# The causal mask of an attention's scores: from a matrix product to a vector addition, with five small edits elsewhere

## The chip, the cores and the metric

One core of a Trainium2 chip runs the whole kernel. The metric is device time in microseconds (us) of one execution, start to end. A core has a matrix engine (TensorE, "PE" in the profile; its weight loads are "PEld"), a vector engine (VectorE, "DVE"), a scalar engine (ScalarE, "ACT"), a general engine (GpSimd, "POOL") and a queue for transfers (SyncE, "SP"). They run side by side and each takes its own instructions in order; semaphores hold an instruction back until what it needs is there. Products are written into eight banks of an accumulator memory, each 128 partitions by 512 float32; the banks are read by VectorE and ScalarE.

## The reference

A decoder layer on 512 tokens of width 1024, in float32: a layer norm of the input, two token mixers side by side (a gated linear attention, GLA, and a multi-head latent attention, MLA), gates and an output projection, a layer norm (LN1), a dense block with a squared ReLU, and a last layer norm (LN2). The change is mainly in the MLA's scores:

```python
for blk in range(seq // Q_BLOCK):                     # 4 blocks of 128 queries
    q0, q1 = blk * Q_BLOCK, (blk + 1) * Q_BLOCK
    s = (jnp.einsum('bhqd,bhkd->bhqk', q_nope[:, :, q0:q1], k_nope[:, :, :q1])
         + jnp.einsum('bhqr,bkr->bhqk', q_rope[:, :, q0:q1], k_rope[:, :q1]))
    s = s.astype(jnp.float32) * scale
    mask = (q0 + jnp.arange(Q_BLOCK))[:, None] >= jnp.arange(q1)[None, :]
    p = jax.nn.softmax(jnp.where(mask, s, -jnp.inf), axis=-1).astype(v.dtype)
    outs.append(jnp.einsum('bhqk,bhkv->bhqv', p, v[:, :, :q1]))
...
h = layer_norm(DEEPNORM_ALPHA * h + mix, ln1_g[l], ln1_b[l])
ff = jnp.square(jax.nn.relu(h @ w_ff1[l])) @ w_ff2[l]
h = layer_norm(DEEPNORM_ALPHA * h + ff, ln2_g[l], ln2_b[l])
```

There are 8 heads, with 128 columns without and 64 with rotation. Only the last 128 columns of a block's scores, its own diagonal, need a mask.

## The kernel before

To keep the precision of float32, each operand of a product is split into a high part and a residual (names ending in hi and lo, or h and l), and a product is made of three: high x high, high x low, low x high. `split` (L109) makes an operand's parts: ScalarE copies the high part, VectorE subtracts it from the source. Weights go through `fetch` (DMA on SyncE's queue into `wraw`) and `pump` (L177), which splits the next weight tile on ScalarE (L189) and VectorE (L190); `weights` calls `pump` ahead of its use. `gemm_fm` (L245 to L247) and `gemm_tm` (L278 to L280) are the products; at half of their evictions `gemm_tm` also calls `pump` for the next matrix (L292, L293).

The order on each engine is not written out by hand. The program is recorded as a stream with generators (`spawn`, `tick`, `finish`) that interleave side work with the products, and a scheduler with a timeline model then fixes the order of each engine. `tc.issue_after(x)` makes an instruction stand behind x in that order.

The stages that the change touches, with their lines:

- Head. `load_x` brings the first two blocks of 128 token rows; `ln_rows` (L400) makes mean and inverse deviation (`bn_stats` L403, `bn_aggr`, a power on GpSimd L406) and normalises: block 0 on ScalarE with one activation of 1024 columns (L410, after `nmr` on VectorE, L409), block 1 on VectorE (L412). `ln_transpose` (L414) transposes 128x128 pieces on TensorE (L421) into banks and applies gain and bias (L424, L426, L428), which gives `h`, the operand of every projection.
- Queries. `mla_qr` (L813) projects four heads' rotary parts with `gemm_tm`; `ev_qr` evicts each of four row blocks by `rope` (three VectorE operations, L498 to L500, and an addition on GpSimd, L501). `y_gla` follows, whose first weights are split meanwhile.
- Scores. `mla_head` (L859), once for each head: for each of four query blocks five products into a bank `px` (L871 to L875; at least 256 columns wide, `nn`), and a sixth, L876, of a bfloat16 identity with the bfloat16 mask `negb`, which adds the mask to the diagonal 128 columns. Then a row maximum (L878, VectorE), the exponential with its sum (L881, ScalarE), reciprocal and normalisation (L882, L883, VectorE). The normalised block is transposed on TensorE (L895) and split, and L914 to L916 multiply it with the values. Two heads of a pair run staggered, only heads 6 and 7 together. There are four `px` banks for all of this.
- LN1. `residual1` (L1193) multiplies the normalised rows `res` by the gain (L1199, L1203) and adds the bias (L1204), on VectorE, for the residual of the dense block. Later, accumulating DMAs from GpSimd's queue (L1305) add the products of the dense block's second half onto `res`. Loads of its second weights stand in the same queue (L1231).
- Tail. The last row block's products (L1413 to L1415) come as 512, 256 and 256 columns; each is added to the residual (L1417) and given to `bn_stats` (L1419). `ln2` (L1208) then aggregates, makes the power on GpSimd (L1217), centres and scales (L1220, L1221) in two halves of 512 columns and sends each half out.

Of the kernel before, what the change touches and what calls it, by code (L numbers as in the profile page):

```python
# [12 lines left out]
BF = mybir.dt.bfloat16  # L13
# [3 lines left out]
ALU = mybir.AluOpType  # L17
# [35 lines left out]
def tile_hybrid_block(ctx: ExitStack, tc: tile.TileContext, I, out, dbg=None):  # L53
# [33 lines left out]
    def MM(n="mm"):  # L87
        return pm.tile([P, T], F32, tag="mm", name=nm(n))
# [43 lines left out]
    mhalf = consts.tile([P, 8], F32, name="mhalf")  # L132
    nc.vector.memset(mhalf, -0.5)
    identr = consts.tile([P, P], F32R, name="identr")
    identb = consts.tile([P, P], BF, name="identb")
    negb = consts.tile([P, P], BF, name="negb")


    stream = []
# [260 lines left out]
    def ln_rows(src, dst, mv, on_act=False):  # L400
        bst = S([P, 2, 6], F32, "bst")
        for j in range(2):
            nc.vector.bn_stats(bst[:, j, :], src[:, j * T:(j + 1) * T])  # L403
        nc.vector.bn_aggr(mv, bst)
        vts(mv[:, 1:2], mv[:, 1:2], LN_EPS, None, op0=ALU.add)  # L405
        gtt(mv[:, 1:2], mv[:, 1:2], mhalf[:, 0:1], op=ALU.pow)  # L406
        if on_act:
            nmr = S([P, 1], F32, "nmr")
            stt(nmr, mv[:, 0:1], -1.0, mv[:, 1:2], op0=ALU.mult, op1=ALU.mult)  # L409
            act(dst, src, AF.Identity, scale=mv[:, 1:2], bias=nmr)  # L410
        else:
            vts(dst, src, mv[:, 0:1], mv[:, 1:2], op0=ALU.subtract, op1=ALU.mult)  # L412

# [21 lines left out]
    hT = []  # L435

    def ln_in0():
        for tt in range(2):
            ln_rows(xt[tt], xt[tt], mvin[:, tt, :], on_act=tt == 0)
        yield from ln_transpose(xt, g_in, b_in, hT, 0, alt=True)  # L440

    pump(-1)
# [1 line left out]


    act(identr, ident, AF.Copy)
    act(identb, ident, AF.Copy)
    cb = consts.tile([P, PACK_B], F32, name="cb")
    nc.scalar.dma_start(cb, I["c_pack_b"])
    cut = np.cumsum([0, 3, 2, NK, GH, 2 * NK, NK, NK, P, 32]).tolist()  # L450
# [14 lines left out]
    def prep():  # L465
        with tc.issue_after(last_in.ins):
            vts(hbg, bgt, 0.5, None, op0=ALU.mult)
            nc.vector.tensor_copy(negb, neg)
            nc.vector.tensor_copy(lmask, lmi)
        posf = consts.tile([P, NT], F32, name="posf")  # L470
        with tc.issue_after(last_in.ins):
            nc.vector.tensor_copy(posf, posi)
        ang = B([P, NT, 32], F32, "ang")
        for tt in range(NT):
            vts(ang[:, tt, :], invf, posf[:, tt:tt + 1], None, op0=ALU.mult)
        yield
        angs = []
        for sh in (0.0, 0.25):
            kq = B([P, NT, 32], F32, "kq")
            vts(kq, ang, 1.0 / (2.0 * math.pi), sh, op0=ALU.mult, op1=ALU.add)  # L480
            vts(kq, kq, MAGIC, None, op0=ALU.add)
            vts(kq, kq, MAGIC, None, op0=ALU.subtract)
            r = B([P, NT, 32], F32, "rr")
            stt(r, kq, -TWO_PI_1, ang, op0=ALU.mult, op1=ALU.add)
            stt(r, kq, -TWO_PI_2, r, op0=ALU.mult, op1=ALU.add)
            stt(r, kq, -TWO_PI_3, r, op0=ALU.mult, op1=ALU.add)
            vts(r, r, sh * 2.0 * math.pi, PI_F, op0=ALU.add, op1=ALU.min)
            vts(r, r, -PI_F, None, op0=ALU.max)
# [324 lines left out]
    def mla_qr(g):  # L813
        qst = []

        def ev_qr(a, j, ps):
            src = ps[:, :4 * ROPE].rearrange("p (h c) -> p h c", c=ROPE)
            csb = cs2[:, a, None, :].to_broadcast([P, 4, ROPE])
            snb = sn2[:, a, None, :].to_broadcast([P, 4, ROPE])
            t1 = B([P, 4, ROPE], F32, "rt1")  # L820
            t2 = B([P, 4, ROPE], F32, "rt2")
            rope(src, csb, snb, t1, t1, t2)
            q2 = B([P, 4, 2, ROPE], F32R, "q2")
            split(t1, q2[:, :, 0, :], q2[:, :, 1, :], scale=scale)
# [12 lines left out]
        return spawn(tr())  # L837
# [21 lines left out]
    def mla_head(h, hl, qn, kn, vt):  # L859
# [4 lines left out]
        P02 = B([P, T], F32, "P02")  # L864
        for i in range(NT):
            n = P * (i + 1)
            nn = max(n, 2 * P)
            c = slice(i * P, (i + 1) * P)
            p = PX()
            o = p[:, :nn]  # L870
            mm(o, qn[:, 0, c], kn[:, 0, :nn], start=True, stop=False)  # L871
            mm(o, qn[:, 0, c], kn[:, 1, :nn], start=False, stop=False)
            mm(o, qn[:, 1, c], kn[:, 0, :nn], start=False, stop=False)
            mm(o, qs[:, c], KK[:, 0, :nn], start=False, stop=False)
            mm(o, qs[:, c], KK[:, 1, :nn], start=False, stop=False)  # L875
            mm(p[:, c], identb, negb, start=False, stop=True)  # L876
# [316 lines left out]
    def residual1():  # L1193
        bg, bb = bcast_row("ln1_g"), bcast_row("ln1_b")
        yield
        with tc.issue_after(st["ln"][1].ins):
            vts(bg, bg, ALPHA, None, op0=ALU.mult)
            vts(bb, bb, ALPHA, None, op0=ALU.mult)
            vtt(res[0], res[0], bg, op=ALU.mult)  # L1199
        yield  # L1200
        for tt in range(NT):
            if tt:
                vtt(res[tt], res[tt], bg, op=ALU.mult)  # L1203
            vtt(res[tt], res[tt], bb, op=ALU.add)  # L1204
            yield


    def ln2(tt, bst=None):  # L1208
# [6 lines left out]
        nc.vector.bn_aggr(mv, bst)  # L1215
        vts(mv[:, 1:2], mv[:, 1:2], LN_EPS, None, op0=ALU.add)
        gtt(mv[:, 1:2], mv[:, 1:2], mhalf[:, 0:1], op=ALU.pow)  # L1217
        for j in range(2):
            c = slice(j * T, (j + 1) * T)
            stt(r[:, c], r[:, c], mv[:, 0:1], bg[:, c], op0=ALU.subtract, op1=ALU.mult)  # L1220
            stt(r[:, c], r[:, c], mv[:, 1:2], bb[:, c], op0=ALU.mult, op1=ALU.add)  # L1221
            nc.sync.dma_start(out[tt * P:(tt + 1) * P, c], r[:, c])
        yield
# [115 lines left out]
    for ci in range(FC):  # L1339
# [34 lines left out]
        else:  # L1374
# [29 lines left out]
            gemm_tm(PL["f2last"], hid, T, ev_res, tts=(2,))  # L1404
            spawn(ln2(2))
            tt, r, bst = 3, res[3], S([P, 4, 6], F32, "bst4")
            for c0, n in ((0, T), (T, 256), (T + 256, 256)):
                acc = MM()[:, :n]
                ws = slice(c0 % T, c0 % T + n)
                for k in range(nb):  # L1410
                    hi, lo = weights(PL["f2last"][c0 // T], k)
                    xh, xl = hid[k][:, 0, tt * P:], hid[k][:, 1, tt * P:]
                    mm(acc, xh, hi[:, ws], start=k == 0, stop=False)  # L1413
                    mm(acc, xh, lo[:, ws], start=False, stop=False)
                    mm(acc, xl, hi[:, ws], start=False, stop=k == nb - 1)  # L1415
                    tick(None)
                vtt(r[:, c0:c0 + n], acc, r[:, c0:c0 + n], op=ALU.add)  # L1417
                for j in range(c0 // 256, (c0 + n) // 256):
                    nc.vector.bn_stats(bst[:, j, :], r[:, j * 256:(j + 1) * 256])  # L1419
            finish(spawn(ln2(3, bst)))  # L1420


# [46 lines left out]
```

## Time and profile before

| what | value |
|---|---|
| median of 3 runs | 896.48 us (896.37 to 897.16) |
| the profiled execution's own time | 896.5 us |
| its span, first to last instruction | 894.7 us |
| mean granted TensorE clock | 0.998 |
| PE busy | 877.5 us, 98%, 4796 instructions |
| PEld busy | 760.5 us, 85% |
| DVE busy | 614.5 us, 69%, 1003 instructions |
| ACT busy | 445.1 us, 50%, 757 instructions |
| POOL busy | 170.4 us, 19%, 190 instructions |
| L876, mask product, 128x128 bf16 | 32 times, 230 ns each |
| L1204, bias of LN1 on VectorE | 4 times 128x1024 |

How to read the profile: times are us from the span's start. A row of a timeline has the start, the length, the engine, the line, the operation and what it writes and reads; "x2" stands for two merged instructions, and the bracket at the end tells how long the engine had been idle and what ended that. TensorE's products overlap in a pipeline, so the length of one is not what it costs; the distance from its start to the next one's is. A row of the waits says which engine and line waited for which, in total, how often, and the longest. The chain of waits goes back from the last instruction, at each step to what released it.

### The profile page before, as it was taken

The page shows a single profiled execution, that of the slowest core. Times are in us where ns is not written, and L with a number is a line of the kernel's source. Part 1 is how long each engine was busy: PE and PEld are TensorE (multiplying, and loading weights), DVE is VectorE, ACT ScalarE, POOL GpSimd, SP SyncE. Part 2 cuts the span into 40 slices and gives each one's busy share as a digit, 9 for nine tenths or more (in the row PEclk, how much of TensorE's full clock was granted, in tenths as well). Part 3 has the DMA queues.
Part 4 walks back from the last instruction along what each step waited for, and adds up shares of the span by engine and source line. Part 5 has one row for each costly group of instructions (what it writes and reads, how often), then busy time and mean ns, then how long its engine had stood idle before and what let it go on. Part 6 is the DMA issues. An engine that isn't in the chain of part 4 may idle for free.

```text
span 894.7 us, 12542 instructions
## 1 busy us (share of the span) xinstructions
PE 877.5 (98%) x4796; PEld 760.5 (85%) x4796; DVE 614.5 (69%) x1003; ACT 445.1 (50%) x757; POOL 170.4 (19%) x190
## 2 busy tenths in 40 slices
PE   6999999999999999999999999999999999999996
PEld 5988888888889988888888888988888888889986
DVE  7835855577775745747756797997556646787866
ACT  6455543443546543535645423366457546656810
POOL 1003442444531010100000002103400520141000
PEclk9999999999999999999999999999999999999999
DMA  7314413216325723112207618004950991399312
GB/s 246 122 47 163 131 60 95 71 48 152 84 71 175 197 87 102 49 55 58 95 25 260 210 48 305 3 0 118 314 135 3 271 257 35 76 231 236 117 62 82
DMA packets 73037, 109.41 MB, mean 122 GB/s; under 512 B 7904, under 2 KB 42080, under 8 KB 72976
## 3 DMA queue, kind: packets, MB, share of 16 engines
q1 hardware_dynamic: 57520, 76.62, 27.1%
q0 software_dynamic: 13536, 28.32, 13.8%
q10 hardware_dynamic: 1920, 3.66, 1.2%
q8 instruction: 38, 0.62, 0.3%
q14 instruction: 23, 0.19, 0.1%
HBM read 91.28 MB, written 4.72 MB: 107 GB/s over the span
## 4 chain that ended last, share of the span: by engine, by line
PE 97%; DVE 1%; DMA 1%; ACT 0%; issue 0%; DVEq 0%
PE mm L245 12%; PE mm L247 12%; PE mm L246 12%; PE mm L278 7%; PE mm L279 7%; PE mm L280 7%; PE mm L1030 3%; PE mm L1029 3%; PE mm L1028 3%; PE px L1288 2%; PE px L1287 2%; PE px L1286 2%; PE px L738 2%; PE mm L1288 2%; PE mm L1287 2%; PE mm L1286 2%
## 5 line engine op out<-in xcount | busy, mean ns | idle before, releaser
L190 DVE TENSOR_TENSOR wlo<-wraw,whi 128x1024 fp32r<-128x1024 f32 (+1 forms) x98 | 110.4, 1127 | 110.0 <-ACT whi L189 102.4
L189 ACT ACTIVATE whi<-wraw 128x1024 fp32r<-128x1024 f32 (+1 forms) x98 | 93.9, 959 | 97.9 <-PE mm L246 48.9
L245 PE MATMUL mm<-h,whi 128*128 128x512 f32 x288 | 112.7, 392 | 0.0
L246 PE MATMUL mm<-h,whi 128*128 128x512 f32 x288 | 112.4, 390 | 0.0
L247 PE MATMUL mm<-h,wlo 128*128 128x512 f32 x288 | 107.1, 390 | 0.0
L1305 POOL DMA_DIRECT2D res<-ev x42 | 37.4, 1003 | 177.9 <-ACT ev L1303 143.6
L245 PEld LDWEIGHTS mm<-h,whi 128*128 128x128 f32 x288 | 54.0, 188 | 11.0
L246 PEld LDWEIGHTS mm<-h,whi 128*128 128x128 f32 x288 | 54.1, 188 | 10.8
L247 PEld LDWEIGHTS mm<-h,wlo 128*128 128x128 f32 x288 | 53.9, 188 | 11.0
L279 PE MATMUL mm<-wlo,h 128*128 128x512 f32 x128 | 50.3, 393 | 0.0
L280 PE MATMUL mm<-whi,h 128*128 128x512 f32 x128 | 50.1, 392 | 0.0
L190 DVE TENSOR_TENSOR wlo<-wq,whi 128x1024 fp32r<-128x1024 f32 x30 | 36.7, 1225 | 19.4 <-ACT whi L189 19.4
L278 PE MATMUL mm<-whi,h 128*128 128x512 f32 x128 | 49.7, 403 | 0.0
L677 POOL TENSOR_TENSOR rp<-rp 128x256 f32<-128x256 f32 x32 | 31.6, 988 | 61.1 <-ACT E L682 44.8
L189 ACT ACTIVATE whi<-wq 128x1024 fp32r<-128x1024 f32 x30 | 31.7, 1058 | 19.7 <-PE mm L1029 11.4
L189 ACT ACTIVATE xh<-wraw 128x1024 fp32r<-128x1024 f32 (+1 forms) x28 | 27.4, 984 | 27.8 <-PE mm L280 16.3
L684 DVE TENSOR_TENSOR M<-E,qk 128x512 f32<-128x512 f32 x32 | 27.8, 868 | 14.1 <-ACT E L682 14.1
L406 POOL TENSOR_TENSOR mv<-mv,mhalf 128x1 f32<-128x1 f32 x4 | 4.6, 1155 | 172.3 <-DVE mv L405 172.3
L190 DVE TENSOR_TENSOR xl<-wraw,xh 128x1024 fp32r<-128x1024 f32 (+1 forms) x28 | 31.3, 1130 | 8.5 <-ACT xh L189 8.4
L1028 PE MATMUL mm<-sh,whi 128*128 128x256 f32 x128 | 36.2, 283 | 0.0
L1029 PE MATMUL mm<-sh,whi 128*128 128x256 f32 x128 | 36.2, 283 | 0.0
L1030 PE MATMUL mm<-sh,wlo 128*128 128x256 f32 x128 | 36.2, 283 | 0.0
(419 smaller groups left out, 2576.9 us busy)
## 6 DMA issues: line engine op xcount, KB each, us to landing
wraw<-in_w_in_dram SPq DMA_DIRECT2D x38, 512.0 KB, 3.5
wraw<-in_w_ff_dram SPq DMA_DIRECT2D x36, 512.0 KB, 5.1
wq<-in_w_ff_dram POOLq DMA_DIRECT2D x26, 512.0 KB, 9.7
res<-ev POOLq DMA_DIRECT2D x42, 256.0 KB, 9.2
wraw<-in_w_o_gla_dram SPq DMA_DIRECT2D x8, 512.0 KB, 3.7
wraw<-in_w_o_mla_dram SPq DMA_DIRECT2D x8, 512.0 KB, 3.5
wraw<-in_w_out_dram SPq DMA_DIRECT2D x8, 512.0 KB, 3.8
wq<-in_w_in_dram SPq DMA_DIRECT2D x6, 512.0 KB, 6.1
```

The source lines that it names most:

```text
L189: st["ins"] = act(hi[:, :nk, :n], raw[:, :nk, :n], AF.Copy)
L190: st["lo"] = vtt(lo[:, :nk, :n], raw[:, :nk, :n], f(hi[:, :nk, :n]), op=ALU.subtract)
L245: mm(o, hi[:, c], xh, start=first, stop=False)
L246: mm(o, hi[:, c], xl, start=False, stop=False)
L247: mm(o, lo[:, c], xh, start=False, stop=last)
L278: mm(o, xh, hi[:, :n], start=opens, stop=False, skip_group_check=share)
L279: mm(o, xh, lo[:, :n], start=False, stop=False, skip_group_check=share)
L280: mm(o, xl, hi[:, :n], start=False, stop=last, skip_group_check=share)
L1028: mm(oa, hi[:, k, c], xh, start=opens and k == 0 and a == 0, stop=False, skip_group_check=True)
L1029: mm(oa, hi[:, k, c], xl, start=False, stop=False, skip_group_check=True)
L1030: mm(oa, lo[:, k, c], xh, start=False, stop=k == 3, skip_group_check=True)
L1305: nc.gpsimd.dma_start(res[tt + t][:, j * T:(j + 1) * T], e, accum_op=ALU.add)
```

## The change

The mask is added by VectorE in the bank: `negb`, `identb` and the sixth product go, and one `tensor_tensor` adds the float32 mask `neg` onto the diagonal 128 columns of the bank before the maximum is taken. As the bank's 128 columns beside the first block no longer need to be opened for it, the products are as wide as the block: 128 columns for the first one instead of 256.

Five small edits stand beside it:

- Head: the normalisation of row block 0 is two activations of 512 columns, and the statistics of row block 1 stand behind `nmr` in VectorE's order.
- Queries: the next weights are split (`pump`) before the first rotation, and the rotations stand behind the residual of these weights on VectorE.
- LN1: the bias is added by an accumulating DMA on GpSimd's queue in place of VectorE.
- LN2: for every row block the centring comes for all columns before the scaling.
- Tail: the last 256 columns of the last row block are copied into a bank by ScalarE ahead of time and the products are accumulated on top; statistics and centring read the bank, and the addition L1417 falls away for these columns. The centring of this block is 768 and 256 columns.

```diff
@@ ln_rows
-            stt(nmr, mv[:, 0:1], -1.0, mv[:, 1:2], op0=ALU.mult, op1=ALU.mult)
-            act(dst, src, AF.Identity, scale=mv[:, 1:2], bias=nmr)
+            end = stt(nmr, mv[:, 0:1], -1.0, mv[:, 1:2], op0=ALU.mult, op1=ALU.mult)
+            for j in range(2):
+                c = slice(j * T, (j + 1) * T)
+                act(dst[:, c], src[:, c], AF.Identity, scale=mv[:, 1:2], bias=nmr)
+            return end
@@ ln_in0
-        for tt in range(2):
-            ln_rows(xt[tt], xt[tt], mvin[:, tt, :], on_act=tt == 0)
+        end = ln_rows(xt[0], xt[0], mvin[:, 0, :], on_act=True)
+        with tc.issue_after(end.ins):
+            ln_rows(xt[1], xt[1], mvin[:, 1, :])
@@ the constants
-act(identb, ident, AF.Copy)
-            nc.vector.tensor_copy(negb, neg)
@@ mla_qr
+            if a == 0:
+                pump(PL["qr", g]["idx"][-1] + 1)
             t1 = B([P, 4, ROPE], F32, "rt1")
             t2 = B([P, 4, ROPE], F32, "rt2")
-            rope(src, csb, snb, t1, t1, t2)
+            with tc.issue_after(st["lo"].ins):
+                rope(src, csb, snb, t1, t1, t2)
@@ mla_head
             n = P * (i + 1)
-            nn = max(n, 2 * P)
...
-            o = p[:, :nn]
-            mm(o, qn[:, 0, c], kn[:, 0, :nn], start=True, stop=False)
-            mm(o, qn[:, 0, c], kn[:, 1, :nn], start=False, stop=False)
-            mm(o, qn[:, 1, c], kn[:, 0, :nn], start=False, stop=False)
-            mm(o, qs[:, c], KK[:, 0, :nn], start=False, stop=False)
-            mm(o, qs[:, c], KK[:, 1, :nn], start=False, stop=False)
-            mm(p[:, c], identb, negb, start=False, stop=True)
+            o = p[:, :n]
+            mm(o, qn[:, 0, c], kn[:, 0, :n], start=True, stop=False)
+            mm(o, qn[:, 0, c], kn[:, 1, :n], start=False, stop=False)
+            mm(o, qn[:, 1, c], kn[:, 0, :n], start=False, stop=False)
+            mm(o, qs[:, c], KK[:, 0, :n], start=False, stop=False)
+            mm(o, qs[:, c], KK[:, 1, :n], start=False, stop=True)
+            vtt(p[:, c], p[:, c], neg, op=ALU.add)
@@ residual1
-            vtt(res[tt], res[tt], bb, op=ALU.add)
+            nc.gpsimd.dma_start(res[tt], bb, accum_op=ALU.add)
@@ ln2
+        w = T if end is None else D - 256
+        for src, c in ((r[:, :w], slice(0, w)), (r[:, w:] if end is None else end, slice(w, D))):
+            stt(r[:, c], src, mv[:, 0:1], bg[:, c], op0=ALU.subtract, op1=ALU.mult)
         for j in range(2):
             c = slice(j * T, (j + 1) * T)
-            stt(r[:, c], r[:, c], mv[:, 0:1], bg[:, c], op0=ALU.subtract, op1=ALU.mult)
             stt(r[:, c], r[:, c], mv[:, 1:2], bb[:, c], op0=ALU.mult, op1=ALU.add)
@@ the tail
+            end = PX()[:, :256]
+            with tc.issue_after(st["ins"].ins):
+                act(end, r[:, D - 256:], AF.Copy)
             for c0, n in ((0, T), (T, 256), (T + 256, 256)):
-                acc = MM()[:, :n]
+                last = c0 > T
+                acc = end if last else MM()[:, :n]
...
-                    mm(acc, xh, hi[:, ws], start=k == 0, stop=False)
+                    mm(acc, xh, hi[:, ws], start=k == 0 and not last, stop=False, skip_group_check=last)
...
-                vtt(r[:, c0:c0 + n], acc, r[:, c0:c0 + n], op=ALU.add)
-                for j in range(c0 // 256, (c0 + n) // 256):
-                    nc.vector.bn_stats(bst[:, j, :], r[:, j * 256:(j + 1) * 256])
-            finish(spawn(ln2(3, bst)))
+                if not last:
+                    vtt(r[:, c0:c0 + n], acc, r[:, c0:c0 + n], op=ALU.add)
+                    acc = r[:, c0:c0 + n]
+                for j in range(n // 256):
+                    nc.vector.bn_stats(bst[:, c0 // 256 + j, :], acc[:, j * 256:(j + 1) * 256])
+            finish(spawn(ln2(3, bst, end)))
```

In the order that the scheduler makes of it, SyncE's queue is the same as before. GpSimd's has the four new DMAs between the powers of LN1's second half (L406) and the first L1305, and one load of L1231 two places later. VectorE has the additions in front of the maxima, often two ahead of two maxima, and the two weight residuals of the queries (L190) ahead of the four rotations. On TensorE some transposes of the second two row blocks stand earlier among the first projection's products, and those of the queries and of the normalised scores stand elsewhere between the same neighbours.

More of the change, by code (lines that the diff above doesn't have):

```diff
@@ L134, in tile_hybrid_block @@
     identr = consts.tile([P, P], F32R, name="identr")
-    identb = consts.tile([P, P], BF, name="identb")
-    negb = consts.tile([P, P], BF, name="negb")
     stream = []
@@ L1203, in residual1, with ln2 @@
                 vtt(res[tt], res[tt], bg, op=ALU.mult)
-            vtt(res[tt], res[tt], bb, op=ALU.add)
+            nc.gpsimd.dma_start(res[tt], bb, accum_op=ALU.add)
             yield
-    def ln2(tt, bst=None):
+    def ln2(tt, bst=None, end=None):
         mv = S([P, 2], F32, "mv")
@@ L1412, in tile_hybrid_block @@
                     xh, xl = hid[k][:, 0, tt * P:], hid[k][:, 1, tt * P:]
-                    mm(acc, xh, hi[:, ws], start=k == 0, stop=False)
-                    mm(acc, xh, lo[:, ws], start=False, stop=False)
-                    mm(acc, xl, hi[:, ws], start=False, stop=k == nb - 1)
+                    mm(acc, xh, hi[:, ws], start=k == 0 and not last, stop=False, skip_group_check=last)
+                    mm(acc, xh, lo[:, ws], start=False, stop=False, skip_group_check=last)
+                    mm(acc, xl, hi[:, ws], start=False, stop=k == nb - 1, skip_group_check=last)
                     tick(None)
-                vtt(r[:, c0:c0 + n], acc, r[:, c0:c0 + n], op=ALU.add)
-                for j in range(c0 // 256, (c0 + n) // 256):
-                    nc.vector.bn_stats(bst[:, j, :], r[:, j * 256:(j + 1) * 256])
-            finish(spawn(ln2(3, bst)))
+                if not last:
[4 more added lines that the diff above has]
+            finish(spawn(ln2(3, bst, end)))
 _FLAT = {
```

## The prediction

> **What bounds the kernel now.** I read the chain of waits first, then what TensorE waited for, then the timelines around every edit.
>
> ```profile
> PE 97%; DVE 1%; DMA 1%; ACT 0%; issue 0%; DVEq 0%
> ...
> PE px L421 <- ACT x L410: 8.3, 1, 8.3
> PE px L738 <- DVE SD L694: 0.5, 1, 0.5
> PE mm L247 <- DVE wlo L190: 0.5, 1, 0.5
> PE mm L278 <- ACT h L424: 0.4, 1, 0.4
> PE mm L245 <- ACT h L424: 0.3, 1, 0.3
> ```
>
> The first row is the chain by engine: TensorE is 97% of it. The others are all of TensorE's waits (total, times, longest). Its first product starts at 8.29, its last ends at 887.64, and in between it waited 1.7 us. So only three things can shorten the run: fewer TensorE slots, those waits, and the head and tail, where TensorE doesn't work. Relief for another engine is worth nothing unless TensorE waits for it.
>
> **Mask product (L876).** TensorE's timeline, start and length:
>
> ```profile
> 355.16 0.28 PE L875 MATMUL px<-KK,QS 128*128 128x256 f32 x1
> 355.28 0.23 PE L876 MATMUL px<-negb,identb 128*128 128x128 bf16 x1
> 355.32 0.36 PE L872 MATMUL px<-qn,qn 128*128 128x256 f32 x1
> 355.52 0.28 PE L873 MATMUL px<-qn,qn 128*128 128x256 f32 x1
> 355.64 0.28 PE L874 MATMUL px<-KK,QS 128*128 128x256 f32 x1
> ```
>
> Lengths overlap, so the cost is start to start. A 256-wide product holds the engine 0.12 (355.52 to 355.64). The mask product holds it 0.04, but the one behind it then takes 0.20 instead of 0.12. All 32 are alike: 0.039, plus 0.083 to 0.088 on the next (0.20 for 0.12, 0.257 for 0.174, 0.314 for 0.227). Price 0.122 each, 32 x 0.122 = 3.9 us. If the second part were something the follower pays anyway, only 32 x 0.039 = 1.2 would go: that is the lower bound. I take 3.9, since followers of three widths all show the same surplus.
>
> **Narrower first block.** For i = 0 the five score products go from 256 to 128 columns, in 8 heads. The trace has 128-wide products of this type in L914 to L916:
>
> ```profile
> 479.05 0.22 PE L914 MATMUL px<-PT,mv 128*128 128x128 f32 x1
> 479.11 0.27 PE L915 MATMUL px<-PT,mv 128*128 128x128 f32 x1
> 479.22 0.28 PE L916 MATMUL px<-PT,mv 128*128 128x128 f32 x1
> 479.33 0.45 PE L914 MATMUL px<-PT,mv 128*128 128x512 f32 x1
> 479.62 0.39 PE L915 MATMUL px<-PT,mv 128*128 128x512 f32 x1
> ```
>
> The first takes 0.06, each further 0.11, and the next wide one 0.29 instead of 0.227. So five cost 0.06 + 4 x 0.112 + 0.06 = 0.57 against 5 x 0.12 = 0.60: 8 x 0.03 to 0.04 = 0.3 us. Half the columns don't halve the time.
>
> [...]
>
> **The addition on VectorE.** The same addition isn't in the trace. Nearest is L499 (128x128, one operand in a bank): 0.28 us, 0.20 start to start. So VectorE gets 32 x 0.20 to 0.28 = 6.4 to 9.0 us more between 350 and 485, where it is busy 88.6 of 135 us. The densest place:
>
> ```profile
> 455.00:470.00 15.00, 15.00 (x90) 12.53 (x88) 10.39 (x32) 7.52 (x24) 0.00 (x0) 1.00 0.01 1
> ```
>
> (Columns: stretch; its length; busy us of PE, PEld, DVE, ACT, POOL.) Heads 6 and 7 run together there: 8 additions make VectorE 12 to 12.6 of 15. Queued behind an addition are the maximum (L878), then reciprocal, normalisation and the weight splits (L190, 1.22); ScalarE's exp (L881) waits for the maximum and TensorE's transposes (L895) for the normalisation. Cover: from 350 to 485, comparing each product's start with the end of the vector work it needs, the least margin is 0.6 us (a bank reused at 455.99), a few are 0.7 to 1.2, most 2 to 4; exp to next use of its bank is 1.2 at 458.14, otherwise 1.4 and more. A block gets 0.2 to 0.28 later and no longer waits for the 0.12 mask. I take 0 for the stalls, bounds 0 and 2 us.
>
> **Queries.** At 320.03 VectorE rotates the first row block (L498 to L500, 0.74) before the weight residual that TensorE waits for:
>
> ```profile
> 320.77 2.89 DVE L190 TENSOR_TENSOR wlo<-wraw,whi 128x1024 fp32r<-128x1024 f32 x2
> ...
> 322.04 0.73 PE L247 MATMUL mm<-ogT,wlo 128*128 128x512 f32 x2 [0.51 <-DVE wlo L190]
> ```
>
> Its ScalarE half ends at 320.25, so the residual can start at 320.28 and end 0.49 earlier. I take 0.49 (bounds 0 and 0.51). The rotations now wait for two residuals, but all of that VectorE work was ahead of the later row blocks already; the next product needing their banks starts 2.3 us after the rotation that frees one (326.72). In group 1 TensorE never waits: 0.
>
> **Tail.** After the last product:
>
> ```profile
> 887.67 0.42 DVE L1417 TENSOR_TENSOR res<-mm,res 128x256 f32<-128x256 f32 x1 [1.99 <-PE mm L1415]
> 888.13 0.43 DVE L1419 BATCH_NORM_STATS2 bst<-res 128x6 f32<-128x256 f32 x1
> 888.60 0.26 DVE L1215 BATCH_NORM_AGGREGATE mv<-bst 128x2 f32<-128x24 f32 x1
> ```
>
> The addition (0.46 start to start) goes: the residual is already in the bank. Statistics then read the bank, for which there is no row: a 256-wide maximum from a bank (L878) steps 0.33, so bounds are 0.1 slower and 0.1 faster. The centring becomes 768 + 256 columns instead of 2 x 512; by 0.72 for 512 and 0.474 for 256 from a bank (L795) both pairs make about 1.3. Sum: -0.46 (0.3 to 0.55). The ScalarE copy that preloads the bank (256 columns, 0.42) stands between weight splits at 855 and the last hid copy (856.23), whose reader starts at 866.76; the row it copies has landed at 825.95. Hidden; without that cover it would cost 0.42.
>
> **LN1.** Four VectorE additions of 1.22 at 579 to 585 leave; TensorE waits for nothing there: 0. Four 512 KB accumulating DMAs join GpSimd's queue between the LN1 powers and the first L1305, where it idles:
>
> ```profile
> 613.72 1.85 POOL L1305 DMA_DIRECT2D res<-ev  x2 [49.81 <-ACT ev L1303]
> ```
>
> Queued 256 KB ones land 1.75 apart, so these need 4 x 3.5 plus some 5, from 580 to about 600; the first reader is at 613.7 and the slice 582 to 604 moves almost nothing. SyncE's order is unchanged; one weight load swaps places with two L1305. Uncovered, each 512 KB would delay the next L1305 by 3.5.
>
> **Head.** The x copy in halves and the earlier nmr bring the first transposes from 8.29 to about 7.4. But the first real product (11.62) follows h (L424), which stands on ScalarE behind three weight copies, the last waiting for a DMA that lands at 10.29. That stays: 0. Row block 1 is normalised some 0.4 later, which those 11.11 hide. Transposes of tokens 256 to 511 move forward, where margins are 0.2 to 1.4: bounds -0.4 and +0.5. The two bf16 casts removed (0.29, 0.22) fill idle time.
>
> **Sum.** 3.9 + 0.3 + 0.49 + 0.46 = 5.15 us. The profiled execution took 896.5 (span 894.7 and 1.8 around it), the median of the runs is 896.48, so nothing has to be shifted: 896.5 - 5.1 = **891.4**.
>
> **Rivals.**
> - VectorE late in the dense places (17%): some blocks around 431 and 455 to 467 use up their 0.6 to 1.2 and TensorE stalls 2 us in all: 893.4. For: the narrow margins. Against: most are 2 to 4.
> - The head improves (11%): until 14.0 a 360-wide product steps 0.30, from then 0.165. If earlier transposes end that slow phase sooner, at most half of 11.62 to 14.0 is won, 1.2: 890.2. Against: products there also wait for evictions with margins of 0.14 to 0.44.
> - The surplus behind the mask stays with another product (8%): only 1.2 + 0.3 + 0.49 + 0.46 = 2.5 goes: 894.0. This is "it doesn't do what it says". Against: the three widths.
> - Slower (6%): every block becomes a wait of TensorE, because the bank goes product, addition, maximum, exp, and four banks don't suffice. Price 0.28 per block and more where a 1.22 split stands ahead; with 0.44 in all 32, 14 us against 5.1: 905. It decides from 0.16 per block, where the gain is gone. Against: today no block makes TensorE wait.
>
> **Chances.** Forecast 58%, its own range 890.6 to 892.4. Range 889.8 to 893.9: it leaves out slower and most of the third rival. Within 0.2% (1.8 us) is what one can't tell from no change. The forecast, the first two rivals and part of the third lie below 894.7: faster 88%, same 6%, slower 6%.
>
> **What would show it.** No L876 on TensorE; after each score group the next product steps 0.12, 0.17 or 0.23; TensorE busy about 4 us less; 32 additions of 0.2 to 0.3 us on VectorE; no L247 wait near 322; statistics right behind the last product, 0.46 sooner; four GpSimd DMAs landed before 610. Wrong if TensorE waits for exp, the transposes or the normalisation between 350 and 480, if the 128-wide score products step 0.2, or if the first product after the head is later than 11.6.

## The result and the profile after

| | median of the runs | against the kernel before, 95% interval |
|---|---|---|
| before, beside it on the same chip | 897.08 us (5 runs, 896.37 to 897.21) | |
| after | 900.87 us (5 runs, 900.15 to 902.27) | 1.0044, 1.0033 to 1.0055 |

The change makes the kernel 0.44% slower, 3.8 us. Forecast were 5.1 us in the other direction. The profiled execution of the changed kernel took 900.8 us, with a span of 899.0.

The chain of waits by engine, from its page, and then the five longest of TensorE's seven waits (total, times, longest; the other two are 0.5 and 0.3):

```profile
PE 95%; DVE 2%; DMA 2%; ACT 0%; issue 0%; POOLq 0%; POOL 0%; DVEq 0%; SPq 0%; ACTq 0%
```

```profile
PE px L422 <- ACT x L410: 7.8, 1, 7.8
PE mm L245 <- DVE wlo L188: 3.3, 1, 3.3
PE px L916 <- DVE PT L112: 1.8, 1, 1.8
PE px L422 <- DVE x L413: 0.9, 1, 0.9
PE px L873 <- DVE PT L112: 0.8, 1, 0.8
```

TensorE still sets the time, but 1.7 us of waiting behind its first product have become 7.6, and transfers stand in the chain with 2%, where they had 1%. The chain in order of time shows where (start, length, what):

```profile
579.54 10.48 DMA res<-bc
590.14 1.23 DVE T L1243
...
593.65 1.15 DVE wlo L188
```

`res<-bc` is the accumulating DMA of LN1 (`bc` is the bias row `bb`, broadcast). The sum `T` on VectorE stands behind it, and the weight residual that TensorE needs stands behind `T`. VectorE's own timeline has the gap as the longest idle time of the stage:

```profile
590.14 1.23 DVE L1243 TENSOR_TENSOR T<-wq,wq 128x1024 f32<-128x1024 f32 x1 [5.52 <-DMA res<-bc]
...
593.56 1.22 DVE L188 TENSOR_TENSOR wlo<-wraw,whi 128x1024 fp32r<-128x1024 f32 x1
```

`T` neither reads nor writes `res`. What ties it to those DMAs is memory. The allocation `A` gives tiles of these names eight buffers in common (L70):

```python
TAG_C = ('h0', 'qn', 'PT1', 'res', 'bc', 'T1', 'T2')
```

The sum gets the buffer of the bias row, and may be written only when the bias row's last reader is done. Before, that was an addition on VectorE itself, ahead of the sum in the same queue, so nothing had to wait. Now it is a transfer that ends at 579.54 + 10.48 = 590.02. With the four additions gone from VectorE, the scheduler has also put the sum ahead of the residual. In the kernel before it stood behind, and the first product with this residual (L247) started at 591.99, 0.5 us after the residual's end:

```profile
590.25 1.23 DVE L190 TENSOR_TENSOR wlo<-wraw,whi 128x1024 fp32r<-128x1024 f32 x1
591.39 1.23 DVE L1239 TENSOR_TENSOR T<-wq,wq 128x1024 f32<-128x1024 f32 x1
```

TensorE's timeline after:

```profile
591.15 0.39 PE L244 MATMUL mm<-h,whi 128*128 128x512 f32 x1
594.84 0.73 PE L245 MATMUL mm<-h,wlo 128*128 128x512 f32 x2 [3.30 <-DVE wlo L188]
...
596.29 0.63 PE L243 MATMUL mm<-h,whi 128*128 128x512 f32 x1
596.72 0.63 PE L244 MATMUL mm<-h,whi 128*128 128x512 f32 x1
...
599.51 0.39 PE L245 MATMUL mm<-h,wlo 128*128 128x512 f32 x1
```

Besides the 3.3 us of waiting there is a second price. From 595.87 to 599.27 a product of 512 columns steps 0.43 instead of 0.227. The granted clock says the same. It is the third number from the end in the busy times by stretch (start and end; length; PE, PEld, DVE, ACT, POOL with their counts; clock; DMA share; GB/s):

```profile
591.00:595.00 4.00, 0.70 (x4) 0.28 (x3) 4.00 (x9) 1.32 (x2) 0.00 (x0) 1.00 0.00 0
595.00:599.30 4.30, 4.30 (x13) 3.36 (x14) 4.30 (x5) 4.30 (x7) 0.00 (x0) 0.60 0.00 0
```

Eight products at 0.43 took 1.6 us more than at 0.227. Together with the wait that is 4.9 of the 5.2 us that TensorE loses here, found by comparing the starts of the same products: 0.6 us ahead of the kernel before at 580, 4.6 behind at 602, and 4.6 still at the last product.

The second loss is in the MLA. ScalarE, then VectorE, then TensorE at the same place, from the timelines of each engine:

```profile
442.56 1.06 ACT L187 ACTIVATE whi<-wraw 128x1024 fp32r<-128x1024 f32 x1
443.53 1.06 ACT L111 ACTIVATE PT<-px 128x512 fp32r<-128x512 f32 x2
```

```profile
443.65 1.23 DVE L188 TENSOR_TENSOR wlo<-wraw,whi 128x1024 fp32r<-128x1024 f32 x1 [0.54 <-ACT whi L187]
444.80 0.29 DVE L878 TENSOR_TENSOR px<-px,cb 128x128 f32<-128x128 f32 x1
445.00 1.28 DVE L112 TENSOR_TENSOR PT<-px,PT 128x512 fp32r<-128x512 f32 x2
```

```profile
445.73 0.50 PE L916 MATMUL px<-PT,mv 128*128 128x512 f32 x1 [1.83 <-DVE PT L112]
```

A weight split stands ahead of the copies of `PT` (the transposed scores, split for the product with the values) on both engines, 1.06 and 1.23 us. In the kernel before the same split stands behind them, as ScalarE's timeline shows:

```profile
442.14 0.60 ACT L111 ACTIVATE PT<-px 128x512 fp32r<-128x512 f32 x1 [1.13 <-PE px L895]
...
443.08 0.60 ACT L111 ACTIVATE PT<-px 128x512 fp32r<-128x512 f32 x1
...
444.78 1.10 ACT L189 ACTIVATE whi<-wraw 128x1024 fp32r<-128x1024 f32 x1
```

The score products of 384 columns just ahead of the wait start 1.7 us earlier than before (442.78 instead of 444.52), the product with `PT` behind it 0.3 us later (445.73 instead of 445.44).

The other edits, in the lines that answer to those of before. The last products of a first block, 128 wide, and behind them a second block's, from TensorE's timeline:

```profile
355.11 0.27 PE L876 MATMUL px<-KK,QS 128*128 128x128 f32 x1
355.22 0.28 PE L877 MATMUL px<-KK,QS 128*128 128x128 f32 x1
355.33 0.33 PE L874 MATMUL px<-qn,qn 128*128 128x256 f32 x1
355.50 0.28 PE L875 MATMUL px<-qn,qn 128*128 128x256 f32 x1
```

128 columns step 0.11, 256 step 0.12, and no product with the mask stands between. Behind a score group the next product follows after 0.11, 0.12, 0.17 and 0.23 (medians of eight by width), without the surplus of 0.08. The queries, on VectorE: the residual now goes ahead of the rotations (L498), and no wait of TensorE is left there.

```profile
321.09 1.23 DVE L188 TENSOR_TENSOR wlo<-wraw,whi 128x1024 fp32r<-128x1024 f32 x1 [3.21 <-ACT whi L187]
...
323.67 0.42 DVE L498 TENSOR_TENSOR rt<-mm,cs 128x256 f32<-128x256 f32 x1
```

The tail, on VectorE: the statistics read the bank right behind the last product, whose start is 891.98.

```profile
892.30 0.43 DVE L1429 BATCH_NORM_STATS2 bst<-px 128x6 f32<-128x256 f32 x1 [0.31 <-PE px L1423]
...
893.13 1.01 DVE L1222 SCALAR_TENSOR_TENSOR res<-res,mv,bc 128x768 f32<-128x768 f32 x1
```

### The profile page after: what moved, and what is told of

Its sections match the earlier page's. It is cut to its first block, busy times and chain, and to the rows that moved or that the text cites. A ratio compares the mean times of both kernels' runs of the same rounds, so it can differ in the third digit from the quotient of the medians.

```text
span 899.0 us, 12510 instructions
## 1 busy us (share of the span) xinstructions
PE 876.7 (98%) x4764; PEld 761.1 (85%) x4764; DVE 615.4 (68%) x1029; ACT 445.6 (50%) x758; POOL 173.2 (19%) x194
## 4 chain that ended last, share of the span: by engine, by line
PE 95%; DVE 2%; DMA 2%; ACT 0%; issue 0%; POOLq 0%; POOL 0%; DVEq 0%; SPq 0%; ACTq 0%
PE mm L243 12%; PE mm L245 12%; PE mm L244 12%; PE mm L276 7%; PE mm L277 7%; PE mm L278 7%; PE mm L1032 3%; PE mm L1031 3%; PE mm L1030 3%; PE px L1292 2%; PE px L1291 2%; PE px L1290 2%; PE px L738 2%; PE mm L1291 2%; PE mm L1292 2%; PE mm L1290 2%
## 5 line engine op out<-in xcount | busy, mean ns | idle before, releaser
L245 PE MATMUL mm<-h,wlo 128*128 128x512 f32 x288 | 108.1, 393 | 3.3 <-DVE wlo L188 3.3
L245 PEld LDWEIGHTS mm<-h,wlo 128*128 128x128 f32 x288 | 54.2, 189 | 14.8 <-DVE wlo L188 3.7
```

The lines of the kernel that those rows point to most:

```text
L245: mm(o, lo[:, c], xh, start=False, stop=last)
```

## The experiments

All medians are us, with the interval of the ratio to the kernel before, run beside them on the same chip (its medians: 897.10, 896.51, 896.85 and 896.65 in the four sets). "Before plus" means the kernel before with that edit alone.

| run | median | ratio, 95% interval |
|---|---|---|
| after, LN1's bias back on VectorE | 895.49 | 0.9987, 0.9978 to 0.9996 |
| after, the sum behind the residual | 895.75 | 0.9988, 0.9979 to 0.9997 |
| before plus LN1 | 901.07 | 1.0042, 1.0029 to 1.0055 |
| before plus mask | 898.98 | 1.0018, 1.0009 to 1.0027 |
| before plus mask, casts kept | 896.84 | 1.0004, 0.9995 to 1.0013 |
| the same without any addition | 892.30 | 0.9956, 0.9944 to 0.9969 |
| the same with an addition of one column | 897.13 | 1.0003, 0.9994 to 1.0012 |
| mask, casts kept, pin | 895.75 | 0.9992, 0.9983 to 1.0001 |
| mask, pin, one more step | 894.10 | 0.9972, 0.9960 to 0.9983 |
| mask in heads 0 to 3 | 895.88 | 0.9988, 0.9979 to 0.9997 |
| before plus head | 896.84 | 1.0001, 0.9992 to 1.0010 |
| head without the order | 900.07 | 1.0034, 1.0021 to 1.0047 |
| mask, pin, queries, tail | 894.32 | 0.9978, 0.9969 to 0.9987 |
| mask in heads 0 to 3, queries, tail | 894.61 | 0.9973, 0.9964 to 0.9983 |
| mask, pin, one more step, queries, tail | 893.10 | 0.9958, 0.9946 to 0.9971 |

### LN1: three runs

The bias back on VectorE, in the changed kernel:

```diff
-            nc.gpsimd.dma_start(res[tt], bb, accum_op=ALU.add)
+            vtt(res[tt], res[tt], bb, op=ALU.add)
```

> The changed kernel with LN1's bias back on VectorE; all else as in the change. Theory A (VectorE's queue stood still from 584.6 to 590.1 because the buffer of the sum T2 is the one the bias row lies in, and the accumulating DMAs read it until they land; TensorE lost 3.3 us by it and about 1.9 us more by slow products behind the stall): 5.2 us of the 900.9 go, about 895.7, and no wait of TensorE of over 0.6 us between 575 and 610. Rival (the 2 MB of transfers or the order of the stage as such cost the time, or the loss lies elsewhere): over 898.5.

The changed kernel with its DMAs, but with the one sum put behind the weight residual in VectorE's order:

```diff
@@ win_sums
-            held(t2, q12, WQ[("f2", ci), ("11", hf)], op=ALU.add)
+            with tc.issue_after(st["lo"].ins) if ci == 0 and hf == 1 else ExitStack():
+                held(t2, q12, WQ[("f2", ci), ("11", hf)], op=ALU.add)
```

> The changed kernel with LN1's bias on the DMAs as in the change, but the waiting sum T2 put behind the weight residual in VectorE's order, so that what waits for the transfers no longer stands ahead of what TensorE needs. Theory A (it is the place in VectorE's queue, not the transfers): as without the DMAs, 895.7, to 896.5 if something behind T2 is late in its turn. Rival (the transfers themselves slow the stage, or the buffer is needed early): over 898.5.

The LN1 hunk of the change alone, on the kernel before:

> The kernel before with the LN1 edit alone. Theory A: the same stall alone, 5.2 us more than before, about 902; VectorE waits some 5.5 us for the transfers ahead of T2, TensorE 3.3 us, and then some 3.4 us of products at 0.43 instead of 0.227. Rival (the stall needs the other edits, since the stage begins at another time): 896.5 to 898.

895.49, 895.75 and 901.07. Taking the DMAs away and leaving them but moving one instruction behind another give the same, 5.4 and 5.1 us below the changed kernel. So it is not the 2 MB of transfers, nor their place on GpSimd's queue: it is the sum that waits at the head of VectorE's queue. In the second run the residual no longer stands behind the sum, and TensorE waits for nothing there:

```profile
589.97 1.23 DVE L188 TENSOR_TENSOR wlo<-wraw,whi 128x1024 fp32r<-128x1024 f32 x1 [0.68 <-ACT whi L187]
...
600.18 1.22 DVE L1243 TENSOR_TENSOR T<-wq,wq 128x1024 f32<-128x1024 f32 x1
```

In the first run the scheduler puts the sum behind the residual by itself (590.69, after the residual at 589.56), so the order of these two goes with the LN1 edit. That the two tiles share a buffer is read from the allocation and from the wait on `res<-bc`; a separate buffer for the bias row wasn't tried.

LN1 alone costs 4.0 us, where 5.2 were expected. Its profiled execution (899.9 us) waited 2.4 us, with VectorE's gap at the same place:

```profile
590.49 1.22 DVE L1239 TENSOR_TENSOR T<-wq,wq 128x1024 f32<-128x1024 f32 x1 [4.61 <-DMA res<-bc]
```

and in this execution no slow products followed: they step 0.227 at once from 595.75 on. The five executions of this kernel took 899.86, 900.18, 901.07, 901.27 and 901.49, with a mean granted clock of 0.998 in the first two and 0.996 in the others. That fits slow products in some and not in others; only the first has a profile. The last section sets such waits side by side.

### The mask: what the addition costs, and why

Before plus the mask hunks of the change:

> The kernel before with the mask on VectorE alone. From the trace of the changed kernel: TensorE gains some 3.4 us between 320 and 444 and gives 2.6 back in two waits for PT, so about 1 us in all: 895.5 to 896.3. Rival (the waits came from the other edits): 892.5 to 893.5, 4 us faster. Second rival (nothing gained): 896.8.

898.98: not 1 us faster but 1.9 slower. In its profile TensorE lost 1.25 us in the head already, where a weight copy had moved ahead of `h` on ScalarE (28.61, the copy of `h` after it at 29.58; with the casts `h` comes at 28.09 and that copy at 28.61). The change had removed two bfloat16 casts, which the scheduler no longer has to place. The next run keeps them, unused (`identb` and `negb`), and with them the head's order:

> The kernel before with the mask on VectorE alone, but with the two unused bfloat16 casts kept, so that the head's order is that of the kernel before (in the mask alone without the casts a weight copy moved ahead of h on ScalarE). Theory A (1.25 us of the mask alone's loss were the head's order): 1 us below the mask alone, about 897.5, with the same waits of TensorE for PT, 1.8 and 0.8. Rival (the head's 1.25 is scatter from run to run): the same as the mask alone, 899.

896.84, or 0.3 above the kernel before it instead of 1.9. Removing two casts that fill idle time had cost about 1.5 us by the medians, through the order that the scheduler then found. The two long waits of the MLA, 1.8 and 0.8, are still there. Now the same kernel without the addition, so without a mask:

```diff
-            vtt(p[:, c], p[:, c], neg, op=ALU.add)
```

> The kernel before without any mask: the sixth product is left out, the products of the first block are 128 wide, and nothing is added on VectorE, so that the scores are not causal. The two bfloat16 casts stay, so that the head keeps its order. Theory A (the mask product costs TensorE 0.122 us, as the prediction priced it, and only VectorE's side takes the gain away): 4.2 us below the kernel before, 892.5 to 893.2, without a wait of TensorE for PT. Rival (the surplus behind the mask product stays, or the narrow products cost more): 1.5 to 2.5 us below, 894.5 to 895.6.

892.30, which is 4.2 below the kernel before, as the mask product and the narrow block had been priced, and TensorE waits for `PT` nowhere (behind its first product it waits for other things, 0.5, 0.5 and 0.3). So the addition on VectorE gives back 4.5 us by the medians. In the profile of the run with the addition the two waits make 2.6 of it, and behind the longer one TensorE runs at about half speed for some 3.4 us (512 columns step 0.42 at 446.29 and 0.23 from 449.78 on), which costs up to 1.7 more. Is it the addition's length? The addition of one column instead of 128:

```diff
-            vtt(p[:, c], p[:, c], neg, op=ALU.add)
+            vtt(p[:, i * P:i * P + 1], p[:, i * P:i * P + 1], neg[:, :1], op=ALU.add)
```

> The kernel before without the sixth product, with the two casts kept, and on VectorE an addition of one column of the 128, so that the scores are not causal. Theory A (it is the length of the addition on VectorE, 0.2 to 0.28 each): near the run without a mask, 892.3 to 893.5, TensorE's waits for PT under 0.5 in all. Theory B (it is the order, and that one more instruction stands in the chain): 894.5 to 896.8, with waits for PT near 429 and 445 as with the whole addition.

897.13, the same as with the whole addition. Its row among VectorE's groups (operation, shape, count, busy us, mean ns), against the changed kernel's:

```profile
L875 DVE TENSOR_TENSOR px<-px,cb 128x1 f32<-128x1 f32 x32 | 5.2, 161 | 6.6 <-PE px L874 6.3
```

```profile
L878 DVE TENSOR_TENSOR px<-px,cb 128x128 f32<-128x128 f32 x32 | 9.2, 292 | 1.8 <-PE px L877 1.8
```

and TensorE's waits in the run with one column, of the same lengths as in the run with the whole addition (1.8 and 0.8):

```profile
PE px L913 <- DVE PT L112: 1.8, 1, 1.8
PE px L870 <- DVE PT L112: 0.8, 1, 0.8
```

The length of the addition is not the main cause: at 55% of it everything stays, where a loss that goes with the length would have shrunk by some 2 us. As one column still takes 161 ns, the run can't say what an addition of no length would do. What also changes with the addition is the order: the splits and the score products of the heads stand elsewhere than in the kernel before, presumably since the scheduler's model sees a chain with one more link. Two runs change the order and leave the whole addition. First, the weight split stands behind the copies of `PT` again in head 4 ("pin"):

```diff
@@ mla_head
-            split(p[:, :n], pt[:, 0, :], pt[:, 1, :])
+            pta = act(pt[:, 0, :], p[:, :n], AF.Copy)
+            pts = vtt(pt[:, 1, :], p[:, :n], f(pt[:, 0, :]), op=ALU.subtract)
...
         omT[h] = om
+        if h == 4:
+            st["gates"] = (pta, pts)
```

> As the run before it, but the weight copy that the scheduler had put ahead of the copies of PT in head 4, and its residual on VectorE, stand behind them again, as in the kernel before. Theory A (TensorE's wait of 1.8 for PT near 445 is this place in ScalarE's and VectorE's order, not VectorE's load; with the slow products that sometimes follow it, it takes 1.8 to 3.4): that wait is gone, 2 to 3 us below the run without the pin, 894 to 895.5. Rival (VectorE is simply too full with the 32 additions): the wait moves to another product, within 0.7 us of the run without the pin.

895.75, 1.1 below the run without it, less than expected. The wait of 1.8 near 445 (on the first product with `PT`, here L914) is 0.2 now, but another is longer:

```profile
PE px L870 <- DVE PT L896: 1.9, 2, 1.1
```

These are first products of a second block (L870), at 429.83 and 455.42, whose bank is still read for `PT`. At the first place they stand directly behind the first block's products, and those directly behind the transposes. In the kernel before, two other products (L247) stood between the two blocks and four (L245, L246) ahead of the first. So one more step between the first and the second block in the recording of heads 4 to 7, which moves both places:

```diff
@@ mla_head, with the pin
-            if i != 0:
+            if i != 0 or h >= 4:
                 yield
```

> The mask on VectorE in all heads with the pin, and in heads 4 to 7 one more step between the first and the second block, so that their score products do not stand directly behind each other on TensorE. Theory A (VectorE's time): no better than the pin alone, 895.5 to 896.5. Theory B (the order): the waits for a bank near 429 and 454 go, 893 to 894.5.

894.10, another 1.7 less, with all the additions in place. The wait at 455 is gone. The other is not: at 429 TensorE waits as long as before, now on the first product with `PT`, the only wait left in the MLA:

```profile
PE px L914 <- DVE PT L896: 0.8, 1, 0.8
```

So two changes of order give back 2.7 of the 4.5 us. The other 1.8 (894.10 against 892.30 without an addition) were not taken apart; that wait of 0.8 is in them.

Last, the mask on VectorE in heads 0 to 3 alone (`vec = h < 4`; the others keep L876 and the wide block):

> The mask on VectorE in heads 0 to 3 alone; heads 4 to 7, where TensorE was seen to wait, keep the sixth product and the wide first block. Theory A (the gain is real where VectorE has room): half of the 4.2 without a new wait, 2.1 below the kernel before, 894.3 to 894.8, so faster than the mask in all heads with the pin (895.75). Rival (the waits come in any head): 895.5 to 896.5.

895.88, where the rival had it. The gain was to be 2.1; in the profile TensorE gained 1.2 between 345 and 485, as a wait of 0.7 came at 429 in head 4, whose two blocks then stood directly behind each other, as with the mask in all heads. So the waits don't need the addition in the head where they come.

### The head: two runs

Before plus the head hunks, and then without the order given to row block 1's statistics:

```diff
-        with tc.issue_after(end.ins):
-            ln_rows(xt[1], xt[1], mvin[:, 1, :])
+        ln_rows(xt[1], xt[1], mvin[:, 1, :])
```

> The kernel before with the head edit alone. Theory A (the statistics of row block 1 stand behind nmr, its x comes 0.9 us after the last transpose of block 0, and this gap makes TensorE's slow start last some 1.3 us longer): 0.6 to 0.9 us slower, 897.1 to 897.5, TensorE waiting 0.9 for x on VectorE. Rival (the head's shift is scatter): the same as before within 0.3. Second rival (the head improves, 1.2 us faster): 895.3.

> The head edit without the order given to row block 1's statistics, only the copy of x in halves. Theory A: the first transposes come earlier, and the gap ahead of block 1 is smaller than 0.9, so no slower than before: 896.2 to 896.8. Rival (the halves alone bring the gap): as the head edit.

896.84, no difference from the kernel before (896.85): my theory of a gap that prolongs the slow start fell, as far as the time goes. The wait of 0.9 is there, and in the profiled execution (897.5, above its median) TensorE is 1.1 behind at 55 us; over 11 executions nothing is left of it. The slow start itself (360 columns step 0.30 in it and 0.165 behind it) ended at another time in each profiled execution: the granted clock reaches 1.00 at 16.66 in this one, and anywhere between 11.33 and 15.25 in the eleven profiled executions with the head of the kernel before, which at 55 us stand between 0.2 us ahead of that kernel's own profile and 0.7 behind it. The copy in halves without the order is 3.2 us slower, against what I expected. Its waits show a new one, on the residual of `h`:

```profile
PE mm L280 <- DVE h L432: 1.9, 1, 1.9
```

### Queries, tail, and the fastest kernel

The edits to the queries and the tail, and with them that to LN2, were added to three versions of the mask:

> The mask with the pin, and with it the edits to the queries and the tail; head and LN1 as before. Theory A (these two give what the trace of the changed kernel shows, 0.48 and 0.36): 0.8 us below the run with the mask and the pin alone, 893.3 to 894.6, about 3 us faster than the kernel before. Rival (the tail gives nothing, since LN1's and the head's edits do not help it): within 0.4 us of the run with the mask and the pin alone.

> The same with the edits to the queries and the tail; head and LN1 as before. Theory A: 0.9 to 1.4 below the run before it, 893.1 to 893.6, the fastest here. Rival (the queries' edit upsets the heads' order): as the run before it or slower.

> The same with the edits to the queries and the tail: 1.3 below the run before it by what these gave twice (1.4 and 1.3). Theory B gives 891.7 to 893.2, the fastest here; theory A 894.2 to 895.2.

894.32, 894.61 and 893.10: 1.4, 1.3 and 1.0 below the same kernels without them. The trace of the changed kernel shows 0.8 for them (0.48 and 0.32, below); with intervals of about 0.9 us to either side the medians can't tell the two apart, and LN2's part has no run of its own. The second lies above its forecast of 893.1 to 893.6 because the run that it builds on did. The last is the fastest here, 0.42% faster than the kernel before (0.29 to 0.54) and 0.9% below the change as it was made: the mask on VectorE with the two casts kept and two places of the order mended, the queries, LN2 and the tail, without the head and LN1 edits.

## Why the prediction was wrong, step by step

- **LN1, the step that decided.** "Four VectorE additions of 1.22 at 579 to 585 leave; TensorE waits for nothing there: 0." The transfers landed sooner than worked out (the last at 590.0, where about 600 was forecast), in an idle stretch and well ahead of the first reader. The error was to look only for readers of what the DMAs write. They also read the bias row, until 590 instead of 585, and the next owner of that buffer is an instruction of VectorE, ahead of work that TensorE needs with 0.5 us to spare (the margin at 591.99 in the kernel before). Cost: 4.0 us alone, 5.1 to 5.4 within the change. No rival had it. It turned a gain into a loss, but without it the change would still have come out at 895.5, 4 us above the forecast; that is the next step's.
- **VectorE's additions.** "I take 0 for the stalls, bounds 0 and 2 us." They cost 4.5, all that the mask product gave. The first rival (stalls in the dense places around 431 and 455 to 467, banks in use) named one of the two places of the changed kernel, the bank at 429, where the wait is 0.8; the longer wait, 1.8 at 445, is at none of its places and for no bank, and its price of 2 was too low. Both the step and this rival reasoned with the length of the addition and with the margins of the old order. The run with one column shows that 45% less length changes nothing; the margins were those of an order that was not kept. Of the 4.5, 2.7 come back with two changes of order; for the other 1.8 the cause stays open. VectorE's load itself came out as estimated: busy 12.5 of 15 us from 455 to 470, in a stretch without the long waits. The order could have been read ahead of the run: the weight copy ahead of `PT` and the sum ahead of the residual stand in the changed program, and the list of moved instructions ahead of the prediction has neither.
- **Mask product and first block.** 3.9 + 0.3 = 4.2; the run without the addition is 4.2 faster by the medians, 2.8 to 5.0 by the interval. 128-wide products step 0.11, as the rows of the profile before had it.
- **The casts.** Their removal was costed at nothing ("fill idle time"). With the mask alone it cost about 1.5 us through the order of the head; in the whole change, which has the head edit too, the trace shows no such loss (for its 0.8 see the head, below).
- **Queries 0.49.** In the trace of the changed kernel TensorE's lag falls from 0.81 at 320 to 0.33 at 322: 0.48. Right.
- **Tail 0.46.** From the end of the last product to the end of the span it was 7.06 (887.64 to 894.7) and is 6.74 (892.26 to 899.0): 0.32, near the lower bound of 0.3. Statistics from the bank start 0.04 after the product's end and take no longer (0.43 in both); the centring takes 1.46 (893.13 to 894.59) instead of the 1.32 of before (888.96 to 890.28). The "about 1.3" for both pairs was a slip: 768 columns at 0.66 per 512 and 0.474 from the bank make 1.46.
- **Head 0.** Right in the median. The trace of the one profiled execution says 0.8, but there the slow start ended at 15.60 instead of 13.99, and half of these 1.61 us is 0.8; the end of the slow start scatters that much with one and the same head.
- **Slower.** It had 6%, and its mechanism, a wait in every block, is not what came. What came was two waits in the MLA and one of 3.3 behind LN1, with slow products behind it. The sign named for a failure there was a wait for the exponential, the transposes or the normalisation between 350 and 480; TensorE waited for the step behind them, the split of the transposed scores.

Summed by the profiles, TensorE's lag from the kernel before to the one after: head +0.8, queries -0.5, MLA -1.0, LN1 +5.2, tail -0.3: +4.2, against 4.3 between the two profiled executions.

## What to carry to other kernels

Where work goes from an engine to a transfer, ask not only who reads what it writes, but how long it now holds what it reads, and who gets that buffer next: here VectorE, waiting 5.52 us for a free buffer, held back the residual behind it and with it TensorE for 3.3. Where a scheduler orders the engines, every edit, a removed cast too, is also an edit to the order; compare the orders of both programs at the places with small margins before adding up durations, and keep the order there by hand. Leave out one part at a time: here the gain (4.2), the loss that the addition brought (4.5, of which 2.7 came back with the order) and the loss by a buffer (5) were each larger than the 3.8 that the sum showed.

## What the runs showed of the hardware

A wait of TensorE cost more than its length in some of the profiled executions. After 3.3 us of waiting the products ran at 0.43 per 512 columns for 3.4 us in the changed kernel. After a wait of 1.83 near 445 the two executions differ: in the changed kernel the clock stayed at 1.00 (products of 512 columns step 0.23 from 446), but in the run with the sum behind the residual, TensorE's timeline and the granted clock were

```profile
446.18 0.50 PE L916 MATMUL px<-PT,mv 128*128 128x512 f32 x1 [1.83 <-DVE PT L112]
...
448.51 0.63 PE L874 MATMUL px<-qn,qn 128*128 128x512 f32 x1
```

```profile
447.20:450.40 3.20, 3.20 (x10) 2.72 (x10) 2.00 (x6) 0.67 (x2) 0.00 (x0) 0.50 0.31 118
```

that is, half speed for some 3.4 us, up to 1.7 us lost, behind a wait of 1.83 us. In the changed kernel the granted clock is 0.50 from 595.86 to 599.27, for 3.41 us.

These are all waits of TensorE above 1.5 us, but for the one ahead of its first product in every execution, and what the trace has behind each:

| profiled execution | wait of TensorE | length | behind it |
|---|---|---|---|
| after, the sum behind the residual | 444.35 to 446.18 | 1.83 | clock 0.50 from 447.20 to 450.40 |
| before plus mask, casts kept | 443.78 to 445.62 | 1.84 | 512 columns step 0.42 at 446.29, 0.23 from 449.78 |
| the same with an addition of one column | 443.48 to 445.30 | 1.82 | clock 0.50 |
| after | 443.90 to 445.73 | 1.83 | clock 1.00 from 446.00 to 449.20 |
| before plus mask | 445.03 to 446.87 | 1.84 | clock 1.00 from 444 to 452 |
| after, LN1's bias back on VectorE | 443.84 to 445.67 | 1.83 | clock 1.00 from 444 to 452 |
| after | 591.54 to 594.84 | 3.30 | clock 0.50 from 595.86 to 599.27 |
| before plus LN1 | 592.80 to 595.18 | 2.38 | 512 columns step 0.23 from 595.75 |
| head without the order | 19.31 to 21.21 | 1.90 | 360 columns step 0.165 from 21.65 |

Half speed came behind 1.82, 1.83, 1.84 and 3.30, and not behind 1.83 (twice), 1.84, 1.90 and 2.38. So the length of a wait alone does not decide it here, and what does is left open. The times of kernels with such a wait lie far apart, 894.7 to 897.6 for the sum behind the residual and 895.2 to 898.5 for the mask with the casts, against 894.0 to 894.9 for the run with one more step; but the mask in heads 0 to 3, whose waits behind the first product are 0.7 and less, has 895.0 to 897.7 too, so the scatter alone shows no cause.
